# The first product on un-normed activations, 1/rms multiplied on behind PSUM

## The chip, the cores and the metric

The kernel runs on one core of a Trainium2 chip. Its time is device microseconds for one launch; a lower one is better. Five engines work on it beside each other, each in the order of its own instruction list: PE (TensorE, matmuls into PSUM), DVE (VectorE), ACT (ScalarE), POOL (GpSimd) and SP, which issues most DMA transfers. They wait for one another by semaphores, and an instruction that waits holds up all that stand behind it on its engine.

## The reference

A token block of 512 tokens with 1024 features goes through a first block (forgetting attention, a state-space branch, memory attention, gated merge) and then through two layers of a second block. What matters here is its beginning:

```python
def rms_norm(x, g):
    xf = x.astype(jnp.float32)
    y = xf * lax.rsqrt(jnp.mean(xf * xf, axis=-1, keepdims=True) + EPS)
    return (y * g.astype(jnp.float32)).astype(x.dtype)

h = rms_norm(x, g_norm[l])
z = h @ w_in[l]
q, k, v, fl, gf, u, gs, qm, gm, gl = split_cols(z)
log_f = jax.nn.log_sigmoid(fl.astype(jnp.float32) + b_forget[l].astype(jnp.float32))
y_s5 = s5_ssm(u, lam_re[l], ...)
```

The 768 columns u of the product feed the state-space branch. The 1/rms of a token is one factor for all features, so (x g) w times 1/rms is the same as (x g / rms) w.

## The kernel before, in words

Everything is feature-major: a tile is 128 features by 512 tokens. The 1024 features of x are eight tiles x[0..7]. Float32 operands are split in two parts, hi (rounded by ACT) and lo (the remainder, by DVE or POOL), and a product is three matmuls for each feature block: hi by hi, hi by lo, lo by hi (`mm3`, L105 to L110). A block of 128 output features so takes 8 x 3 = 24 matmuls of 512 columns.

Weights come in pieces of 128 by 1024 words (0.52 MB). `fetch` (L70) loads a raw piece `wr`, `split` (L79) makes `wh` on ACT (L88) and `wl` on DVE or, for every second piece, on POOL (L90). There are three buffers each of `wr`, `wh` and `wl`, so `wh` of piece n+3 can be written only when PE has read `wh` of piece n for the last time. `get` (L93) splits three pieces ahead and fetches three more. The first block's u needs pieces 0 to 5, one for each of its six output blocks; pieces 6 to 8 are for the product behind it.

The beginning (`block1`, L1457): x arrives in 16 transfers, each half of the tokens of a feature block. ACT squares it, DVE adds the squares up in `sacc` (L175). `rstd` (L192) sums `sacc` over the features with four small matmuls (L181), forms mean + eps on DVE (L199), raises it to -1/2 on POOL (L201) and spreads it over all rows in PSUM by four more (L188). `norm` then makes h: x times g times 1/rms on DVE (`hu`, L551), hi on ACT (L213), lo on DVE (L221), a half of the tokens at a time. `head` (L565) runs the first three u blocks in matmuls of 256 columns (L584, L585, L588), half by half; the other three go through `strip` and `fm` (L112) at 512 columns. `upost` (L1482) copies each block out of PSUM on ACT, reordered (L1484), and sends it through DRAM into the layout of the state-space scan.

Behind the six blocks PE goes on with `forget` (L1341), which needs all of h, and with the attention's `fv` strip (L124 to L126). On DVE the tables of the state-space branch (`s5_setup`, some 120 operations on 128 x 24 tiles, `s5t`, `s5pw`, `s5keep`) are worked in between; ACT has a table load and a sine and cosine of them (L1139, L1140).

The order on each engine is set at build time by a scheduler that merges all of this into five lists by its own estimate of the times. On the chip the lists are fixed. PSUM has eight banks: three `mm` for the blocks of a product, four `s` for small results and one `pv`.

Of the kernel before, what the change touches and what calls it, by code (L numbers as in the profile page):

```python
# [23 lines left out]
def f32(t):  # L24
    return t.bitcast(F32)


class Core:
# [17 lines left out]
    def u(self, dt=F32, name="u"):  # L46
        """a [128, 512] tile of four-byte words from the common ring."""
        self.n += 1
        return self.ring.tile([128, T], dt, tag="u", name=f"{name}_{self.n}", bufs=self.NU)
# [5 lines left out]
    def psum(self, cfg):  # L55
        """(re)divide the eight PSUM banks"""
# [36 lines left out]
    def get(self, name, kb):  # L93
        """the next piece: hi and lo as [128, kb, columns]."""
# [17 lines left out]
    def fm(self, out, w, c0, act, kb):  # L112
        """feature-major block: out[128 features, tokens] from strip columns c0..c0+128."""
        (wh, wl), (ah, al) = w, act
        for k in range(kb):
            self.mm3(out, wh[:, k, c0:c0 + 128], wl[:, k, c0:c0 + 128], ah[k], al[k], k == 0, k == kb - 1)

    def tm(self, out, ws, act, tok, cols=slice(0, 256)):
        """token-major block: out[128 tokens, cols]; ws: pieces that follow one another along k."""
# [34 lines left out]
    @staticmethod  # L154
    def half(t, hf):
        """half of the tokens: of four blocks of 128 in order, two."""
# [3 lines left out]
    def halfp(t, hf):  # L160
        """the first or second half of the tokens, in the order (t mod 4, t div 4)."""
        return t.rearrange("p (r i) -> p r i", r=4)[:, :, 64 * hf:64 * hf + 64]

    def sq_acc(self, xj, j, c=slice(0, T), name="sacc", scale=1.0):
        """sum of squares of the feature blocks, by columns."""
# [11 lines left out]
    def sumcols(self, pq, sacc, cols):  # L177
        """pq[:, i]: sums over features of the tokens of 128-blocks; cols: lists of first columns that add up."""
# [4 lines left out]
    def bcast(self, r):  # L183
        """columns r [128, n] -> [128, n * 128] in PSUM, the same in every row."""
# [7 lines left out]
    def rstd(self, sacc, cols):  # L192
        """broadcast of 1/sqrt(mean + eps), in PSUM."""
# [10 lines left out]
    def hsplit(self, src, bias=None, out=None):  # L204
        """hi, lo of src (+ bias)."""
# [20 lines left out]
class Att(Core):  # L226
    """Softmax attention on split operands. A head's logits come twice: query-major for the row
    maximum, key-major for the weights that multiply V and a block of ones, which sums them."""

    @staticmethod  # L230
    def cut(t, c):
        """columns c of t: a slice, or (i0, i1) for those of the tokens 4 i + r in the order (r, i)."""
# [5 lines left out]
    def byblock(t):  # L238
        """t, tokens 4 i + r in blocks of 128 and within these in the order (r, i), as [p, r, block, i]."""
# [3 lines left out]
    def like(t, c):  # L243
        """t in the shape of the columns c."""
        return t if isinstance(c, slice) else t.rearrange("p (r i) -> p r i", r=4)

    def split3(self, dst, src, nsh):
        """dst[..., i] (bf16, i = 0..2) add up to src (float32)."""
# [15 lines left out]
    def turn(self, mc, psum_tag):  # L264
        """columns [128 tokens, 4, 128] -> rows [128, 512] in PSUM (exact)."""
# [5 lines left out]
    def rows(self, mc, tag, psum_tag, out=None):  # L271
        """the same as bf16 in SBUF; of these the last 32 if out is given."""
# [9 lines left out]
    def unit(self, nh, sregs, tregs, qk, vsl, dst, extra=None, nq=4, hd=64, orow=None, fold=None):  # L282
        """Items of a unit of nh heads (pairs of heads share 128 rows of output).
        sregs(qb): tiles of regions (c0, n, piece, q slice, k slice, mask)
        tregs(): tiles of (regions, [(v piece, kb, columns)])
        fold(j): the tile whose other half takes the rows of -max (else these come by a product of their own)
        qk(j, piece) -> pairs (q, k); vsl(j, piece, kb) -> (hi, lo); dst(j) -> (tile AP rows, row0)"""
# [118 lines left out]
        def vrow(j):  # L406
            """rows of a head's values in its sum; the other half holds the sum of the weights."""
# [41 lines left out]
    def mix(a, b, z=1.0):  # L449
        """a and b as one list, spread evenly, b over the first part z."""  # L450
# [3 lines left out]
    def merge(self, a, b):  # L454
        """run items of a with those of b spread evenly among them."""
# [13 lines left out]
class Blk2(Att):  # L469
    def ada_gen(self, l):  # L470
        """columns [128, 48] of silu(c) @ w_ada[l] + b_ada[l]."""
# [6 lines left out]
        def fin(acc, c):  # L478
            """acc: rows of two parts, c and c + 1"""
# [36 lines left out]
    def load2(self):  # L516
        """constants of the second block"""
# [21 lines left out]
    def norm(self, x, gcols, shcols, h):  # L539
        """by half of the tokens: hi and lo of rms(x) * g + shift. Returns the stages stat, hi, lo."""  # L540
# [24 lines left out]
    def head(self, names, h, posts, norm, view, byw=False):  # L565
        """the first blocks behind a norm, a half of the tokens at a time."""
# [26 lines left out]
    def tail(self, name, act, posts):  # L593
        """the last two blocks before a norm, a half of the tokens at a time."""
# [44 lines left out]
    def put(self, o, isq, dst, scale=None, both=False, byblock=False):  # L639
        """stacks of two heads: q -> [hi;lo]; k -> [hi;hi] and lo in the rows of the head. both: q -> [hi;lo] and hi with  # L640
        the other half left to -max; k -> [hi;hi] and lo with ones for it, for heads of either half."""
# [53 lines left out]
    def pairs(q, k):  # L695
        """operand pairs whose products make up a head's logits"""
# [14 lines left out]
    def block(self, w, c0, act, kb, post):  # L711
        """one feature-major block; post(psum) may return a generator of later stages."""
# [12 lines left out]
    def strip(self, name, act, kb, posts):  # L725
        """items of feature-major blocks."""
# [12 lines left out]
    def v3(self, nb=4):  # L739
        """hi/lo token-major value tiles [128 keys, nb blocks, 128]."""  # L740
        return tuple(self.u(F32R, "v").rearrange("p (b d) -> p b d", b=nb) for _ in range(2))

    def v_new(self):
        """token-major values of two heads, in two tiles of two key blocks: hi as [v0, 1, 1, v1], lo as [v0, 0, 0, v1]."""
# [1287 lines left out]
```

## Time and profile before

| | |
|---|---|
| time, median of 3 runs | 2513.65 us (2512.61 to 2514.68) |
| span of the profiled execution, first to last instruction | 2516.8 us |
| PE busy | 2388.2 us, 95% |
| DVE, ACT, POOL busy | 61%, 41%, 32% |
| DMA | 265.28 MB, mean 105 GB/s |

The profiled execution is one of its own; its span is 3.2 us (0.13%) longer than the median of the timed runs, and its time around the span is not listed. Line numbers are those of the kernel before. In a row of the timeline the first number is the start in us from the span's start, the second the duration; brackets tell how long the engine sat idle and what released it. Matmuls overlap, so the step from one to the next is the difference of their starts, not the duration.

### The profile page before, as it was taken

What the parts mean: (1) busy time and instruction counts of PE and PEld (TensorE: products, weight loads), DVE (VectorE), ACT (ScalarE), POOL (GpSimd) and SP (SyncE); (2) the same over time, 40 slices, a digit from 0 to 9 for tenths busy, and PEclk for the clock granted to TensorE, in tenths of its full rate; (3) what the DMA queues carried; (4) which work ended last, traced back from release to release, by engine and by line L of the source; (5) the groups of instructions that cost most, each with busy time, mean ns of one, the idle gap of its engine ahead of it and who ended that gap; (6) DMA issues with size and microseconds to landing.
All of it is one profiled execution on the core that took longest, in us unless ns stands there. A gap on an engine that the chain in (4) does not pass through costs nothing. (4 is left out here: it accounts for less than half of the span.)

```text
span 2516.8 us, 32068 instructions
## 1 busy us (share of the span) xinstructions
PE 2388.2 (95%) x12162; PEld 1978.9 (79%) x12162; DVE 1533.0 (61%) x2394; ACT 1038.1 (41%) x1639; POOL 812.3 (32%) x601
## 2 busy tenths in 40 slices
PE   7999989989998889999999999998999999999999
PEld 6876778767888777787787888886777777888888
DVE  7667766666998887555459663258864726522222
ACT  4445543452333447533333423433663423423432
POOL 2445354634221552142122121227311612222121
PEclk9999999999998999998899999999999979999999
DMA  5311113213674321121138553233111313222232
GB/s 183 98 47 55 57 61 108 94 59 135 237 264 172 113 76 51 51 85 66 50 102 301 176 209 101 93 114 99 59 51 50 93 34 117 84 94 99 93 101 84
DMA packets 105610, 265.28 MB, mean 105 GB/s; under 512 B 13664, under 2 KB 23408, under 8 KB 105456
## 3 DMA queue, kind: packets, MB, share of 16 engines
q1 hardware_dynamic: 104304, 261.47, 31.2%
q8 instruction: 96, 1.57, 0.3%
q10 hardware_dynamic: 1152, 1.77, 0.2%
q14 instruction: 58, 0.48, 0.1%
HBM read 244.69 MB, written 9.44 MB: 101 GB/s over the span
## 5 line engine op out<-in xcount | busy, mean ns | idle before, releaser
L108 PE MATMUL pmm<-h,wh 128*128 128x512 f32 (+1 forms) x2232 | 855.7, 385 | 14.7 <-ACT h L213 3.9
L110 PE MATMUL pmm<-h,wl 128*128 128x512 f32 (+1 forms) x2232 | 852.9, 382 | 3.7 <-POOL wl L90 2.8
L109 PE MATMUL pmm<-l,wh 128*128 128x512 f32 (+1 forms) x2232 | 853.4, 383 | 0.0
L90 POOL TENSOR_TENSOR wl<-wr,wh 128x1024 fp32r<-128x1024 f32 (+1 forms) x173 | 422.5, 2442 | 1315.4 <-ACT wh L88 1094.4
L88 ACT CAST wh<-wr 128x1024 fp32r<-128x1024 f32 (+1 forms) x346 | 358.2, 1036 | 928.5 <-PE pmm L109 726.4
L108 PEld LDWEIGHTS pmm<-h,wh 128*128 128x128 f32 x2232 | 424.5, 190 | 96.7 <-ACT h L213 4.8
L110 PEld LDWEIGHTS pmm<-h,wl 128*128 128x128 f32 x2232 | 424.5, 190 | 82.5 <-POOL wl L90 3.8
L109 PEld LDWEIGHTS pmm<-l,wh 128*128 128x128 f32 x2232 | 425.2, 191 | 76.5 <-DVE l L221 0.7
L90 DVE TENSOR_TENSOR wl<-wr,wh 128x1024 fp32r<-128x1024 f32 (+1 forms) x173 | 225.1, 1301 | 168.9 <-ACT wh L88 166.5
L383 DVE TENSOR_TENSOR pl<-pe,ph 128x512 fp32r<-128x512 f32 (+4 forms) x168 | 121.7, 733 | 139.7 <-ACT ph L381 138.9
L961 DVE SCALAR_TENSOR_TENSOR x<-pmm,ada,x 128x512 f32<-128x512 f32 (+1 forms) x100 | 64.2, 643 | 213.9 <-PE pmm L110 213.7
L311 PE MATMUL ps<-qk,qk 128*128 128x512 f32 (+4 forms) x416 | 147.9, 386 | 16.1 <-POOL qk L672 9.6
L505 DVE SCALAR_TENSOR_TENSOR adacc<-adw,cact,adacc 128x512 f32<-128x512 f32 x168 | 154.3, 928 | 3.2 <-DMA adw<-in_wada 0.3
L221 DVE TENSOR_TENSOR l<-r,h 128x512 fp32r<-128x512 f32 x64 | 59.3, 928 | 121.6 <-ACT h L213 121.3
L379 ACT ACTIVATE pe<-ps 128x512 f32<-128x512 f32 (+4 forms) x168 | 84.5, 503 | 80.8 <-PE ps L311 72.7
L311 PEld LDWEIGHTS ps<-qk,qk 128*128 128x128 f32 x416 | 83.1, 204 | 37.7 <-POOL qk L672 11.5
L108 PE MATMUL pmm<-yh,wh 128*128 128x512 f32 (+1 forms) x244 | 94.1, 389 | 3.9 <-ACT yh L1403 2.4
L110 PE MATMUL pmm<-yh,wl 128*128 128x512 f32 (+1 forms) x244 | 93.7, 386 | 0.0
L109 PE MATMUL pmm<-yl,wh 128*128 128x512 f32 (+1 forms) x244 | 93.0, 382 | 0.0
L381 ACT CAST ph<-pe 128x512 fp32r<-128x512 f32 (+4 forms) x168 | 88.8, 528 | 9.4 <-DVE pl L383 3.5
L402 PE MATMUL ppv<-pl,v 128*128 128x512 f32 (+2 forms) x216 | 79.0, 366 | 4.1 <-DVE pl L383 4.0
L400 PE MATMUL ppv<-ph,v 128*128 128x512 f32 (+2 forms) x216 | 79.0, 366 | 2.7 <-ACT ph L381 1.6
(365 smaller groups left out, 3863.2 us busy)
## 6 DMA issues: line engine op xcount, KB each, us to landing
wr<-in_w SPq DMA_DIRECT2D x324, 512.0 KB
adw<-in_wada SPq DMA_DIRECT2D x192, 256.0 KB
xs<-xg SPq DMA_DIRECT2D x136, 64.0 KB
wr<-in_w SPq DMA_DIRECT2D x22, 384.0 KB
xd<-x SPq DMA_DIRECT2D x16, 256.0 KB
x<-xd SPq DMA_DIRECT2D x16, 256.0 KB
x<-in_x SPq DMA_DIRECT2D x16, 128.0 KB
x<-in_x SPq DMA_DIRECT2D x8, 256.0 KB
```

What stands on the lines that cost most here:

```text
L88: self.nc.scalar.copy(h[:, 0:n], r[:, 0:n])
L90: eng.tensor_tensor(out=l[:, 0:n], in0=r[:, 0:n], in1=f32(h)[:, 0:n], op=ALU.subtract)
L108: mm(out, wh, ah, start=start, stop=False)
L109: mm(out, wh, al, start=False, stop=False)
L110: mm(out, wl, ah, start=False, stop=stop)
L311: mm(outs[i] if len(r.shape) == 2 else outs[i].rearrange("p (r i) -> p r i", r=r.shape[1]), w, r, start=first and i == 0, stop=last and i ...
L379: nc.scalar.activation(out=e[:, w], in_=pt[:, w], func=AF.Exp)
L381: nc.scalar.copy(ph[:, w], e[:, w])
L383: nc.vector.tensor_tensor(out=pl[:, w], in0=e[:, w], in1=f32(ph)[:, w], op=ALU.subtract)
L400: mm(self.cut(pv, c), vh, h, start=f, stop=False)
L402: mm(self.cut(pv, c), vh, lo, start=False, stop=z)
L505: nc.vector.scalar_tensor_tensor(out=acc, in0=w, scalar=cc, in1=acc, op0=ALU.mult, op1=ALU.add)
```

## The change

x comes in eight transfers of whole feature blocks, with the first three weight pieces fetched between the first of them. From each x block, hi and lo of x times g are made directly (`rh` on ACT, `rl` on DVE), without 1/rms, into 16 tiles of their own. The first three u blocks run on these at full width, feature block by feature block over three PSUM banks of the kind `mm`. Behind them in program text come the statistics, once for all tokens, and a copy `R` of the spread 1/rms from PSUM to SBUF (ACT). `upost` multiplies by `R` as it leaves PSUM, on DVE, in place of ACT's copy. h is made after that, at full width, from x, g and `R`, for all that needs it behind u. The last three u blocks also use the un-normed tiles. The other lines that differ between the two files are comments and doc strings.

```diff
         x = [self.u(name="x") for _ in range(8)]
+        g = self.col("g_norm", 0, 8)
+        raw = [], []
         with self.tc.high_priority():
-            for hf in range(2):
-                for j in range(8):
-                    if 8 * hf + j == self.F0:
-                        self.fetch(0)
-                    nc.sync.dma_start(out=self.half(x[j], hf), in_=self.half(self.a["x"][:, j, :], hf))
-        for hf in range(2):
             for j in range(8):
-                self.sq_acc(self.half(x[j], hf), j, slice(256 * hf, 256 * hf + 256))
+                if j < 3:
+                    self.fetch(j)
+                nc.sync.dma_start(out=x[j], in_=self.a["x"][:, j, :])
+            for j in range(8):
+
+                hi, lo = self.u(F32R, "rh"), self.u(F32R, "rl")
+                nc.scalar.activation(out=hi, in_=x[j], func=AF.Copy, scale=g[:, j:j + 1])
+                self.stt(lo, x[j], g[:, j:j + 1], f32(hi), ALU.mult, ALU.subtract)
+                raw[0].append(hi)
+                raw[1].append(lo)
+        for j in range(8):
+            self.sq_acc(x[j], j)
         h = self.new_h()
-        norm = self.norm(x, self.col("g_norm", 0, 8), None, h)
...
+        R = self.u(name="R")
...
-                nc.scalar.copy(t.rearrange("p (i b) -> p b i", i=4), pm.rearrange("p (b i) -> p b i", i=4))
+                v = lambda z: z.rearrange("p (b i) -> p b i", i=4)
+                self.tt(t.rearrange("p (i b) -> p b i", i=4), v(pm), v(R), ALU.mult)
...
-        self.head(["u"] * 3, h, [upost(j) for j in range(3)],
-                  norm, self.half, True)
-        del x, norm
+        ws = [self.get("u", 8) for _ in range(3)]
+        pms = [self.p("mm") for _ in range(3)]
+        for k in range(8):
+            for (wh, wl), pm in zip(ws, pms):
+                self.mm3(pm, wh[:, k, :], wl[:, k, :], raw[0][k], raw[1][k], k == 0, k == 7)
+        pr = self.rstd(self.sums["sacc"], [[128 * b] for b in range(4)])
+        nc.scalar.copy(R, pr)
+        for j in range(3):
+            self.done(pms[j], upost(j))
+        for j in range(8):
+            t = self.u(name="hu")
+            self.stt(t, x[j], g[:, j:j + 1], R, ALU.mult, ALU.mult)
+            self.hsplit(t, None, (h[0][j], h[1][j]))
...
-        self.merge(self.strip("u", h, 8, [upost(j) for j in range(3, 6)]), [])
+        self.merge(self.strip("u", raw, 8, [upost(j) for j in range(3, 6)]), [])
```

Where it moves instructions, at three places. The number at the end of a name counts tiles and differs between the files.

POOL, the first rows behind its start. `nr` is the -1/2 power of the statistics, `wl` the lower part of a weight piece. Before:

```order
L201 TENSOR_TENSOR nr_62_206<-nv_61_204,mhalf_5_72 128x2
L90 TENSOR_TENSOR wl_76_242<-wr_74_239,wh_75_241 128x1024
L201 TENSOR_TENSOR nr_91_274<-nv_90_272,mhalf_5_72 128x2
L90 TENSOR_TENSOR wl_84_258<-wr_80_251,wh_83_257 128x1024
L90 TENSOR_TENSOR wl_120_517<-wr_82_255,wh_119_516 128x1024
```
and now, where the four `wl` are those of pieces 1, 3, 5 and 7:

```order
L90 TENSOR_TENSOR wl_72_210<-wr_26_122,wh_71_209 128x1024
L90 TENSOR_TENSOR wl_79_224<-wr_75_217,wh_78_223 128x1024
L90 TENSOR_TENSOR wl_118_411<-wr_77_221,wh_117_410 128x1024
L201 TENSOR_TENSOR nr_89_317<-nv_88_315,mhalf_5_72 128x4
L90 TENSOR_TENSOR wl_130_489<-wr_83_233,wh_129_488 128x1024
```
The one `nr` that is left stands behind the splits of pieces 1, 3 and 5; before, the two stood ahead of and behind the split of piece 1.

ACT, around the making of h (L213). Before, the second half of the tokens and the first rows behind it (`wh_83` and `wh_86` are pieces 3 and 4):

```order
L213 CAST h_41_182<-hu_93_359 128x256
L213 CAST h_42_183<-hu_94_362 128x256
L213 CAST h_43_184<-hu_95_365 128x256
L213 CAST h_44_185<-hu_96_368 128x256
L213 CAST h_45_186<-hu_97_371 128x256
L213 CAST h_46_187<-hu_98_374 128x256
L213 CAST h_47_188<-hu_99_377 128x256
L213 CAST h_48_189<-hu_100_380 128x256
L88 CAST wh_83_257<-wr_80_251 128x1024
L1484 COPY us_101_463<-ppv_57_198 128x128x4
L88 CAST wh_86_263<-wr_81_253 128x1024
L1484 COPY us_103_471<-pmm_58_199 128x128x4
```
and now, from the copy of 1/rms on (`wh_123`, `wh_129` and `wh_137` are pieces 6, 7 and 8):

```order
L1505 COPY R_68_204<-ps_90_319 128x512
L88 CAST wh_123_449<-wr_80_227 128x1024
L213 CAST h_52_188<-hu_97_349 128x512
L213 CAST h_53_189<-hu_98_353 128x512
L88 CAST wh_129_488<-wr_83_233 128x1024
L213 CAST h_54_190<-hu_99_357 128x512
L213 CAST h_55_191<-hu_100_361 128x512
L88 CAST wh_137_554<-wr_119_414 128x1024
L213 CAST h_56_192<-hu_101_365 128x512
L213 CAST h_57_193<-hu_102_369 128x512
L213 CAST h_58_194<-hu_103_373 128x512
L213 CAST h_59_195<-hu_104_377 128x512
```
The eight `h` no longer stand together: piece 6 stands ahead of all of them, piece 7 behind the second, piece 8 behind the fourth.

DVE, the lower parts of h (`l`, L221). Before:

```order
L221 TENSOR_TENSOR l_49_190<-hu_93_359,h_41_182 128x256
L221 TENSOR_TENSOR l_50_191<-hu_94_362,h_42_183 128x256
L221 TENSOR_TENSOR l_51_192<-hu_95_365,h_43_184 128x256
L221 TENSOR_TENSOR l_52_193<-hu_96_368,h_44_185 128x256
L221 TENSOR_TENSOR l_53_194<-hu_97_371,h_45_186 128x256
L221 TENSOR_TENSOR l_54_195<-hu_98_374,h_46_187 128x256
L221 TENSOR_TENSOR l_55_196<-hu_99_377,h_47_188 128x256
L1073 SCALAR_TENSOR_TENSOR s5t_181_941<-s5t_181_941,s5t_180_940 128x24
L221 TENSOR_TENSOR l_56_197<-hu_100_380,h_48_189 128x256
```
and now, from the fifth feature block to the end (`wl_138` is piece 8, `us_120` the fourth u block as it leaves PSUM):

```order
L1073 SCALAR_TENSOR_TENSOR hu_101_365<-x_21_115,cols_4_69,R_68_204 128x512
L90 TENSOR_TENSOR wl_138_555<-wr_119_414,wh_137_554 128x1024
L221 TENSOR_TENSOR l_64_200<-hu_101_365,h_56_192 128x512
L1073 SCALAR_TENSOR_TENSOR hu_102_369<-x_22_116,cols_4_69,R_68_204 128x512
L221 TENSOR_TENSOR l_65_201<-hu_102_369,h_57_193 128x512
L1073 SCALAR_TENSOR_TENSOR hu_103_373<-x_23_117,cols_4_69,R_68_204 128x512
L221 TENSOR_TENSOR l_66_202<-hu_103_373,h_58_194 128x512
L1073 SCALAR_TENSOR_TENSOR hu_104_377<-x_24_118,cols_4_69,R_68_204 128x512
L221 TENSOR_TENSOR l_67_203<-hu_104_377,h_59_195 128x512
L1070 TENSOR_TENSOR fll_108_386<-wfl_105_381,flh_107_385 128x4x12
L1070 TENSOR_TENSOR us_121_441<-pmm_120_416,R_68_204 128x128x4
L1070 TENSOR_TENSOR fll_110_392<-wfl_105_381,flh_109_391 128x4x12
```
The lower part of piece 8 stands ahead of the fifth `l`, and the multiplication of the fourth u block stands behind the last `l`.

## Rows read from the trace of the kernel before

**Rows 1.** The page, engines over the whole span: busy us (share) and instructions

```profile
PE 2388.2 (95%) x12162; PEld 1978.9 (79%) x12162; DVE 1533.0 (61%) x2394; ACT 1038.1 (41%) x1639; POOL 812.3 (32%) x601
```

**Rows 2.** Busy time per engine in four stretches; last DMA share and GB/s

```profile
0.00:20.00 20.00, 4.22 (x16) 3.55 (x16) 12.35 (x38) 11.36 (x25) 4.26 (x8) 1.00 0.79 256
...
20.00:40.00 20.00, 20.00 (x147) 20.00 (x147) 17.60 (x73) 8.97 (x17) 3.11 (x2) 1.00 0.19 66
...
0.00:2.00 2.00, 0.00 (x0) 0.00 (x0) 1.17 (x8) 0.34 (x1) 1.19 (x6) 1.00 0.08 8
...
12.00:14.00 2.00, 1.22 (x4) 0.93 (x4) 0.48 (x1) 1.56 (x3) 0.44 (x1) 1.00 1.07 411
```

**Rows 3.** Timeline of PE: start us, duration us, instruction [idle before <-releaser]

```profile
12.50 1.22 PE L188 MATMUL ps<-c,nr 128*128 128x128 f32 x4 [1.04 <-POOL nr L201]
...
25.39 0.41 PE L584 MATMUL pmm<-h,wh 128*128 128x256 f32 x1
...
26.44 0.28 PE L584 MATMUL ppv<-h,wh 128*128 128x256 f32 x1
...
39.87 0.40 PE L108 MATMUL pmm<-h,wh 128*128 128x512 f32 x1
...
56.22 0.39 PE L108 MATMUL pmm<-h,flh 128*128 128x512 f32 x1
```

**Rows 4.** Timeline of PE around a pause later in the program

```profile
560.12 0.80 PE L402 MATMUL ppv<-pl,v 128*128 128x512 f32 x1 [4.01 <-DVE pl L383]
...
562.00 0.63 PE L109 MATMUL pmm<-l,wh 128*128 128x512 f32 x1
...
562.42 0.63 PE L110 MATMUL pmm<-h,wl 128*128 128x512 f32 x1
...
565.22 0.39 PE L108 MATMUL pmm<-h,wh 128*128 128x512 f32 x1
```

**Rows 5.** Timeline of ACT, the first 75 us

```profile
15.21 1.04 ACT L88 CAST wh<-wr 128x1024 fp32r<-128x1024 f32 x1 [0.48 <-DMA wr<-in_w]
...
35.80 1.05 ACT L88 CAST wh<-wr 128x1024 fp32r<-128x1024 f32 x1 [5.74 <-PE ppv L588]
...
41.30 1.28 ACT L1139 ACT_TABLE_LOAD   x1
...
42.73 0.30 ACT L1140 ACTIVATE s5t<-s5t,hpi 128x24 f32<-128x24 f32 x1
```

**Rows 6.** Timeline of DVE, the first 75 us

```profile
16.64 2.33 DVE L175 TENSOR_TENSOR sacc<-sacc,sq 128x256 f32<-128x256 f32 x1
...
38.75 1.67 DVE L90 TENSOR_TENSOR wl<-wr,wh 128x1024 fp32r<-128x1024 f32 x1 [1.84 <-ACT wh L88]
...
44.25 0.39 DVE L1070 TENSOR_TENSOR s5t<-s5keep,s5t 128x24 f32<-128x24 f32 x2
...
48.48 1.23 DVE L90 TENSOR_TENSOR wl<-wr,wh 128x1024 fp32r<-128x1024 f32 x1
...
49.63 0.17 DVE L1070 TENSOR_TENSOR s5pw<-s5pw,s5t 128x24 f32<-128x24 f32 x1
```

**Rows 7.** Timeline of POOL, the first 75 us

```profile
11.74 0.70 POOL L201 TENSOR_TENSOR nr<-nv,mhalf 128x2 f32<-128x2 f32 x1 [10.02 <-DVE nv L199]
...
16.33 2.36 POOL L90 TENSOR_TENSOR wl<-wr,wh 128x1024 fp32r<-128x1024 f32 x1 [3.89 <-ACT wh L88]
...
36.92 2.41 POOL L90 TENSOR_TENSOR wl<-wr,wh 128x1024 fp32r<-128x1024 f32 x1 [14.55 <-ACT wh L88]
```

**Rows 8.** Groups by line and shape: count, busy us, mean ns, idle before

```profile
L1073 DVE SCALAR_TENSOR_TENSOR yl<-yf,yh 128x512 fp32r<-128x512 f32 x6 | 3.7, 684 | 0.0
...
L421 DVE TENSOR_TENSOR ym<-ppv,rb 128x512 f32<-128x512 f32 x4 | 2.7, 687 | 1.8 <-PE ppv L402 1.8
...
L213 ACT CAST h<-r 128x512 fp32r<-128x512 f32 x64 | 39.8, 621 | 2.0
...
L1484 ACT COPY us<-pmm 128x512 f32<-128x512 f32 x5 | 5.3, 1103 | 0.0
```

## The prediction, made before the changed kernel was run

> **What bounds the kernel now.** I read the page first: PE is busy 95% of the span [rows 1], so the time is PE's work plus the places where PE stands. Then the stretches: in the first 20 us PE works 4.22 us, in the next 20 all 20 [rows 2]. The change lies in this beginning, up to PE's first matmul of the forget product, the first reader of h behind u. I use that matmul as the mark: it starts at 56.22 us, and 72 matmuls earlier, at 39.87, the first three u blocks are done [rows 3]. These 72 run without a gap, 0.227 us apart. Whatever the change does to the mark passes on to the end, as PE is the bound from there on and all that follows needs h. So I sum to the mark, in the profiled execution's time, and put the difference on the median. Third, PE's timeline for its two speeds: matmuls of 256 columns take 0.41 us until 25.4 and 0.28 from 26.4 [rows 3]. It happens again later: behind a pause of 4.01 us the 512-column matmuls stand 0.42 us apart, which is 1.2 GHz, and at 565.2 they are short again (2.4 GHz) [rows 4]. The slow stretch is the 5.1 us from 560.12 on less a first matmul of 0.8: 4.3 us, ten steps of 0.42, each 0.2 too long. A pause of this length costs 2.0 us besides itself.
>
> **Removed, on PE.** 144 matmuls of half width become 72 of full width: by the step of 0.227 us, 16.35 us. Half the columns in half the step is the same work, and I cost the width itself at nothing. One of two rounds of statistics goes. The 16 half transfers of x become 8, ACT's squares run at full width under PE's first product: nothing on the path. ACT no longer copies u (1.1 us each [rows 8]); DVE does.
>
> **The first three blocks.** They no longer wait for statistics, but ACT's first `rh` stands behind the cast of weight piece 1. In front of and with that piece come 1.50 MB: two pieces of 0.52, one x block of 0.26, constants 0.19. Before, the same piece came with 3.34 MB in front of it or in it, and its cast began at 15.21 [rows 5]; the first 2 us move nothing [rows 2], so 0.255 MB/us, and 8.0 us for it now (5.7 at the 411 GB/s of 12 to 14 us [rows 2], the fast end). Cast 1.04 [rows 5], `rh` 0.62 [rows 8]: PE's first two matmuls at 9.7. The third needs `rl` from DVE. There POOL is in the way: it splits piece 1 from 9.1 to 11.5, and a DVE operation that meets such a split ends only behind it. A 256-column addition that began at 16.64, 0.3 us after POOL had begun at 16.33, took 2.33 us [rows 6, 7]. So `rl` is done at 12.2 (11.5 + 0.68 [rows 8]). Then 70 matmuls follow, the first 12 slow (0.42 each [rows 4], some 5 us as the engine comes from rest), 58 at 0.227: 12.2 + 5.1 + 13.2 = **30.5 us**, 9.4 earlier than 39.87. The last x block, behind 3.9 MB in all, is there at 17, so transfers don't hold it.
>
> **The first stall: R.** The fourth block needs a PSUM bank, and all three `mm` banks hold products that wait for R. On paper R takes 4 us; in the changed order other work stands ahead of it.
> - ACT casts pieces 3, 4 and 5 as buffers come free. All three pieces in use are read to the end now (feature block by feature block), so the first buffer is free 7 matmuls before the end: casts end at 29.95, 31.0, 32.0.
> - POOL splits piece 3 from 30.0 to 32.4 (2.4 each [rows 7]) and piece 5 to 34.8; `nr` stands behind both.
> - DVE's split of piece 4 is locked out until 32.4 (as the one at 38.75, which met POOL's of 36.92 and took 1.67 [rows 6, 7]) and ends at 33.6; then DVE is locked again until 34.8. The statistics' small operation follows at 35.0, `nr` (0.70 [rows 7]) at 35.7, the spreading on PE (1.22 [rows 3]) at 36.9.
> - ACT loads a table (1.28 [rows 5]) and makes sine and cosine by 36.9, too, then copies R: 37.5.
> - DVE has 34 table operations between the cosine and the first multiplication by R. Before, the same ones ran from 44.25 to 49.63 with a split of 1.15 in between [rows 6]: 4.2 us. So the multiplication begins at 41.1 and frees a bank at **41.8** (0.687 from PSUM [rows 8]; ACT's reordering copy took 1.1 [rows 8], the upper bound).
>
> PE pauses 11.3 us but for the small matmuls. Blocks 4 to 6: 16.35 + 2.0 for slow matmuls; they end at 49.25, 54.7 and 60.15.
>
> The Trainium skill ("SBUF — State Buffer", "SBUF: two separate sides") says that whichever of the two engines starts first holds the shared ports for its whole instruction and the other is blocked. The rows bear out one side, DVE behind POOL. By the rule DVE's split of piece 4 at 32.4, if it comes first, would also push POOL's next split, and `nr`, by 1.2 us; the sum would be 1.2 us higher.
>
> **The second stall: h.** h is made from R, from 37.5 on if nothing stood ahead. But on ACT piece 6 is ahead of the first `h`, piece 7 ahead of the third, piece 8 ahead of the fifth, and their buffers are freed by the ends of blocks 4, 5 and 6. (Such casts wait for PE now already: 5.74 us before the one at 35.80 [rows 5], but no `h` stands behind them.) On DVE `hu` and `l` alternate, each `l` waiting for ACT: 0.68 + 0.62 + 0.68 = 2.0 us for each feature block.
> - Piece 6: cast to 50.3, DVE's split to 51.5 (1.23 [rows 6]); `l` 1 and 2 at 53.5 and 55.5.
> - Piece 7: cast to 55.9 at the latest; POOL's split to 58.3 locks DVE: `l` 3 at 59.0, `l` 4 at 61.0.
> - Piece 8: cast from 60.3 to 61.4, split to 62.9; `l` 5 at 63.6, then 65.6, 67.6, 69.6.
>
> The forget product needs besides these the bank of block 4, which DVE frees behind the last `l`: 69.6 + 0.1 + 0.69. The mark is at **70.5**, 14.3 later than 56.22, behind a pause of 10.3 us, so 2.0 more for slow matmuls: **+16.3 us**. Raw weights from piece 12 on stand in SP's queue behind the u transfers of block 6, as before; three split pieces, 16 us of PE's work, cover them. I see nothing that gives the delay back: the later pauses of PE hang on its own products.
>
> On the profiled execution 2516.8 becomes 2533.1; on the median 2513.65 becomes **2530**.
>
> **Bounds.** Down: no slow matmuls behind the pauses (-4), DVE never locked out (-2.3, -2.4, -1.5), faster transfers (-2.3): +4. Up: 1.1 us for the multiplication (+0.8), longer slow phases as at the start (+2), the order of the splits (+1.2): +20. Nearest to the rows is the sum, as pauses of 4 us and locked operations are both in them. Less the fastest corner and with 3 us for a delay further on, 2519 to 2537.
>
> **Rivals.**
> - *R comes at once.* The statistics' chain is 4.4 us by itself (1.0 for the sums, 0.2, 0.7, 1.2, 0.6, 0.7). If nothing stood ahead, blocks 4 to 6 would run from 34.9 to 53.3 and h be ready by 46 (eight times 1.4 on DVE): the mark 2.9 us earlier, 4.9 if PE stays fast, 2509 to 2511. For it: PE's product does start 7 us sooner, and the scheduler's list is no slower than its operations. It decides if `nr` is done by 32.5. Against it: POOL's list, where two splits of 2.4 us stand ahead of `nr`, which none of them needs. 4%, half of it beyond 0.2%.
> - *One stall only.* R late as worked out, but h ready when block 6 ends, at 60.2: +4.0, 2517.6. It needs the casts of pieces 6 to 8 not to wait for PE; with three buffers I see no way, only that all pauses shrink together. 10%.
> - *It spreads.* The forget gates and the attention behind them come 16 us late on three engines, and the scan's u with them; if PE has no other work there, another wait of the 4 us kind [rows 4] with its slow matmuls comes on top twice: +28, 2542. 8%.
>
> **Chances.** The forecast has 78%. 0.2% is 5.0 us, about what a measurement of this kernel can tell from no change. Faster by more: 0.02. Within: 0.08, most of the second rival and the fast corner. Slower: 0.90. The range leaves out the first rival and the third, 12 in 100, and the second's better half.
>
> **What would show it.** In the new profile: PE's first 512-column matmul near 9.7 and the 72nd near 30; a pause of about 11 us whose releaser is DVE's `us`; ACT idle between R and the cast of piece 6 until block 4 ends; a second pause of about 10 us ahead of the matmuls on `flh`, released by DVE; and matmuls 0.42 apart for some 4 us behind both. A first pause under 6 us, or `h` made in one run ahead of piece 6, would prove me wrong, and so would a mark before 60.

## The result

The changed kernel took 2545.52 us (median of 4 runs, 2537.02 to 2545.94), the kernel before 2513.43 beside it: a ratio of 1.0119, interval 1.01 to 1.0137. It is slower, as forecast, but by 32 us and not by 16.3, outside the range of 2519 to 2537. Three more jobs of the same kernel gave 1.0123, 1.009 and 1.0113; in the means of the four jobs it stood 30.0, 32.5, 21.8 and 26.0 us above the kernel before. Over all jobs 22 runs of it have a mean of 2542.6 (standard error 1.4) and 115 runs of the kernel before one of 2515.1 (0.7): 27.5 us.

Single runs scatter: those of the kernel before lie between 2495.3 and 2529.4 us, and with them goes the granted clock averaged over the run (2502.58 us at 0.977, 2529.38 at 0.961; correlation -0.95, 1.9 us for 0.001). The traces of both kernels belong to runs that were a few us longer than these means (spans of 2516.8 and 2543.0 us, 26.2 apart). So places are compared in traces, and times as means.

**The profile after.** PE's timeline, the answer to [rows 3]:

```profile
9.35 1.23 PE L108 MATMUL pmm<-rh,wh 128*128 128x512 f32 x2 [9.35 <-ACT rh L1477]
11.72 0.79 PE L109 MATMUL pmm<-rl,wh 128*128 128x512 f32 x1 [1.15 <-DVE rl L1073]
...
30.54 0.95 PE L181 MATMUL ps<-c,sacc 128*128 128x1 f32 x8
37.23 2.08 PE L188 MATMUL ps<-c,nr 128*128 128x128 f32 x8 [5.75 <-POOL nr L201]
43.57 0.77 PE L108 MATMUL pmm<-rh,wh 128*128 128x512 f32 x1 [4.26 <-DVE s5pb L1183]
...
62.08 0.39 PE L110 MATMUL pmm<-rh,wl 128*128 128x512 f32 x1
73.07 0.77 PE L108 MATMUL pmm<-h,flh 128*128 128x512 f32 x1 [10.60 <-DVE fll L1070]
73.63 0.63 PE L109 MATMUL pmm<-l,flh 128*128 128x512 f32 x1
...
79.18 0.41 PE L110 MATMUL pmm<-h,fll 128*128 128x512 f32 x1
```

The first three blocks are done at 30.54, 9.3 us earlier than before. Then PE stands twice: from 30.5 to 43.57 but for the small matmuls, and 10.60 us ahead of the mark, which comes at 73.07 against 56.22: 16.85 us later. Behind it 13 steps of 0.427 us (73.63 to 79.18) cost 0.2 each, 2.6 us. The releasers named (`s5pb`, `fll`) are neighbours in DVE's list: the first stands two rows behind the multiplication `us` of the first block, the second one row behind that of the fourth (`us_121` of the list shown with the change).

ACT in the same stretch, the answer to [rows 5]:

```profile
29.15 2.94 ACT L88 CAST wh<-wr 128x1024 fp32r<-128x1024 f32 x3 [10.45 <-PE pmm L109]
...
36.22 1.28 ACT L1139 ACT_TABLE_LOAD   x1
...
39.35 0.58 ACT L1505 COPY R<-ps 128x512 f32<-128x512 f32 x1 [1.41 <-PE ps L188]
51.45 1.05 ACT L88 CAST wh<-wr 128x1024 fp32r<-128x1024 f32 x1 [11.51 <-PE pmm L109]
54.45 0.62 ACT L213 CAST h<-hu 128x512 fp32r<-128x512 f32 x1 [1.96 <-DVE hu L1073]
...
62.53 1.04 ACT L88 CAST wh<-wr 128x1024 fp32r<-128x1024 f32 x1
...
70.52 0.62 ACT L213 CAST h<-hu 128x512 fp32r<-128x512 f32 x1 [1.42 <-DVE hu L1073]
```

Behind `R` ACT stands for 11.51 us: piece 6 waits for block 4, and the first `h` stands behind piece 6. The last `h` comes at 70.52, 31 us behind `R`.

DVE, the answer to [rows 6]:

```profile
31.18 2.54 DVE L90 TENSOR_TENSOR wl<-wr,wh 128x1024 fp32r<-128x1024 f32 x1 [3.05 <-ACT wh L88]
33.64 2.31 DVE L1067 TENSOR_SCALAR s5t<-s5t 128x24 f32<-128x24 f32 x1
...
42.40 1.02 DVE L1070 TENSOR_TENSOR us<-pmm,R 128x512 f32<-128x512 f32 x1
...
59.19 2.12 DVE L221 TENSOR_TENSOR l<-hu,h 128x512 fp32r<-128x512 f32 x1 [0.69 <-ACT h L213]
...
71.90 1.02 DVE L1070 TENSOR_TENSOR us<-pmm,R 128x512 f32<-128x512 f32 x1
```

A table operation of 0.17 us takes 2.31 and an `l` of 0.69 takes 2.12: both met a split on POOL. POOL itself, the answer to [rows 7], and behind it the two splits of its first row by themselves (shortest, median and longest, in ns):

```profile
30.28 5.63 POOL L90 TENSOR_TENSOR wl<-wr,wh 128x1024 fp32r<-128x1024 f32 x2 [19.16 <-ACT wh L88]
36.17 1.01 POOL L201 TENSOR_TENSOR nr<-nv,mhalf 128x4 f32<-128x4 f32 x1 [0.26 <-DVE s5keep L1067]
58.20 2.56 POOL L90 TENSOR_TENSOR wl<-wr,wh 128x1024 fp32r<-128x1024 f32 x1 [21.02 <-ACT wh L88]
...
L90 POOL TENSOR_TENSOR wl<-wr,wh x2: 2352/2840/3327, 30.3 to 32.6; 128x1024 fp32r<-128x1024 f32 x2
```

The clock in four stretches of 10 us (the column of 0.74, 0.58, 0.78 and 0.54 is PEclk):

```profile
30.00:40.00 10.00, 3.56 (x20) 3.06 (x18) 7.90 (x33) 4.61 (x8) 6.64 (x3) 0.74 0.43 157
40.00:50.00 10.00, 6.43 (x18) 5.18 (x19) 6.08 (x27) 0.00 (x0) 0.00 (x0) 0.58 0.14 46
...
60.00:70.00 10.00, 2.47 (x11) 1.70 (x10) 7.95 (x11) 3.42 (x5) 4.65 (x13) 0.78 0.57 200
70.00:80.00 10.00, 6.93 (x18) 5.48 (x19) 4.42 (x8) 0.88 (x3) 0.00 (x0) 0.54 0.27 85
```

It falls in each pause, and PE comes out of both at 1.2 GHz: steps of 0.427 us last until 48.4 behind the first and until 79.2 behind the second.

So the beginning explains 16.85 + 2.6 = 19.4 us. The other 8 of the 27.5 lie further on. From the mark to the end, before and after:

```profile
56.22:2516.80 2460.58, 2347.80 (x11931) 1941.96 (x11929) 1489.97 (x2226) 1009.71 (x1586) 796.18 (x578) 0.97 0.31 104
...
73.07:2543.00 2469.93, 2355.26 (x11930) 1948.06 (x11930) 1494.02 (x2227) 1007.90 (x1584) 796.22 (x577) 0.96 0.31 103
```

The first number behind the comma is PE's busy time: the same matmuls take it 7.5 us more (2.6 of them the slow steps just named), and it stands idle 1.9 us longer. There the two programs have the same text, yet the scheduler made the lists anew: on PE they differ in three stretches (in the trace of before those at 202 to 225, 930 to 957 and 1781 to 1830 us), on ACT, DVE and POOL in a few places each.

### The profile page after: what moved, and what is told of

Same layout as the page of the kernel before. It is cut to its first block, busy times and chain, and to the rows that moved or that the text cites. A ratio compares the mean times of both kernels' runs of the same rounds, so it can differ in the third digit from the quotient of the medians.

```text
span 2543.0 us, 31897 instructions
## 1 busy us (share of the span) xinstructions
PE 2397.2 (94%) x12090; PEld 1981.7 (78%) x12090; DVE 1545.0 (61%) x2384; ACT 1035.0 (41%) x1626; POOL 812.9 (32%) x600
## 4 chain that ended last, share of the span: by engine, by line
PE 50%; DVE 7%; issue 4%; POOL 2%; ACT 2%; DMA 2%; SPq 1%; DVEq 0%; POOLq 0%; ACTq 0%
PE pmm L108 13%; PE pmm L109 13%; PE pmm L110 13%; PE ps L311 4%; DMA adw<-in_wada 1%; PE ppv L402 1%; PE ppv L400 1%; PE ppv L401 1%; POOL wl L90 1%; DVE unm L336 1%; DVE xs L624 1%; PE ps L617 1%; DVE adacc L505 1%; DVE wl L90 0%; POOL qv L620 0%
## 5 line engine op out<-in xcount | busy, mean ns | idle before, releaser
L110 PE MATMUL pmm<-h,wl 128*128 128x512 f32 (+1 forms) x2208 | 844.3, 383 | 3.8 <-POOL wl L90 2.8
L221 DVE TENSOR_TENSOR l<-r,h 128x512 fp32r<-128x512 f32 x64 | 59.3, 928 | 121.6 <-ACT h L213 121.3
L379 ACT ACTIVATE pe<-ps 128x512 f32<-128x512 f32 (+4 forms) x168 | 84.5, 503 | 86.5 <-PE ps L311 79.2
L336 DVE TENSOR_REDUCE unm<-ps 128x1 f32<-128x512 f32 (+2 forms) x112 | 65.0, 596 | 29.6 <-PE ps L311 29.2
```

Of the source, the lines that this page charges most:

```text
L110: mm(out, wl, ah, start=False, stop=stop)
L336: nc.vector.tensor_reduce(out=nm, in_=pts[0], axis=AX.X, op=ALU.max, negate=True)
L379: nc.scalar.activation(out=e[:, w], in_=pt[:, w], func=AF.Exp)
```

## The experiments

Each ratio is to the kernel before, run in turn with it. Line numbers of the variants are shifted by up to 18.

**r_first: the statistics first**

```diff
+        with self.tc.high_priority():
+            (sq_acc of all x, rstd)      # traced ahead of the weights
+            lead = (the sums' nv on DVE, nr on POOL)
+            nc.scalar.copy(R, pr)
+        self.lead = {i: lead for i in (3, 4, 5)}   # these splits are queued behind lead
...
-        self.s5_setup()
+        (s5_setup queued behind the third us on DVE)
```

> The changed kernel with the statistics put ahead: the sums and the power stand ahead of the splits of pieces 3 to 5 on DVE and POOL, and the state-space tables behind the first three multiplications by R. Theory (two stalls in a row, the second set by pieces 6 to 8 standing ahead of h): R at 30 to 31 instead of 39.4, PE restarts near 36 instead of 43.6, but h still waits for the ends of blocks 4 to 6, with the tables now in front of it as well, so the mark stays where it was, 71 to 75 us against 73.07, and the time at 2540 to 2547. Rival (the late R is the whole delay): the mark comes 6 to 8 us earlier, the time 2538 or less.

Ratio 1.0084 (1.0052 to 1.0116). PE:

```profile
33.64 0.47 PE L120 MATMUL pmm<-rh,wh 128*128 128x512 f32 x1 [1.85 <-DVE us L1082]
70.43 0.77 PE L120 MATMUL pmm<-h,flh 128*128 128x512 f32 x1 [20.18 <-DVE fll L1082]
```

`R` came at 31.83 and PE restarted 10 us earlier, but all except 2.6 us of that turned into a longer second pause of 20.18. R alone is not the delay. The edit made part of this pause itself: the tables now stand between the steps of h on DVE, and one of their operations took 6.29 us (45.77 to 52.06) while POOL split piece 7 and cleared tiles. The time, 2537.43 in the median, fell below the 2540 to 2547 that the theory gave.

**h_first: pieces 6 to 8 behind h**

```diff
             self.hsplit(t, None, (h[0][j], h[1][j]))
+        lead = (the last l on DVE, the last h on ACT)
+        self.lead.update({i: lead for i in (6, 7, 8)})
```

> The changed kernel with pieces 6, 7 and 8 put behind the last h on ACT and DVE, nothing else. Theory (two stalls): the first pause stays (PE restarts at 43 to 44), h is made in one run while blocks 4 to 6 are worked on, and only the weights of piece 6 and what POOL locks are left: the mark at 65 to 69 us instead of 73.07, the second pause 3 to 6 us instead of 10.6, the time 2537 to 2542. Rival (h is late only because R is): mark and time stay within 1 us.

Ratio 1.0031 (1.0008 to 1.0053), mark at 64.82:

```profile
43.10 0.76 PE L120 MATMUL pmm<-rh,wh 128*128 128x512 f32 x1 [4.26 <-DVE s5pb L1195]
64.82 0.77 PE L120 MATMUL pmm<-h,flh 128*128 128x512 f32 x1 [3.07 <-DVE us L1082]
```

With the first pause as it was, three pieces put behind h bring 8.3 us. The second stall is the order of pieces and `h`, not a late `R`. The time gained more than the mark: its mean of 2527.8 is 14.7 us below that of the changed kernel, and its median of 2525.87 lies well below the 2537 to 2542 expected.

**both: the two together**

> Both of the orders of the two kernels before it. Theory: the gains add up only now, the mark at 61 to 65 us, still later than the 56.22 of the kernel before the change since PE waits for wl of piece 3 (all three pieces end together) and DVE has h, three multiplications and splits locked by POOL in a row: time 2530 to 2536. On the loss behind the mark (9 us more between the two profiles): if it goes with the pauses and the clock behind them, this kernel loses under 5 us behind the mark against the kernel before; if it comes of the order that the scheduler gives the later program, it has no reason to shrink and may be anything from -3 to +10.

Ratio 1.001 (0.9985 to 1.0035), restart at 34.06, mark at 62.53. The mark gains only 2.3 us more than in h_first: PE now waits 11.86 us, since table operations stand between the steps of h on DVE, and behind the last `l` (done at 57.6) a split and a table operation that met POOL's split of piece 7 (59.10, 2.33 us) stand ahead of the multiplication that frees the bank. The time was again lower than the 2530 to 2536 expected.

**nr_first: of r_first only the statistics**

> Of the kernel r_first only the first half: the statistics' sums and power ahead of the splits, the state-space tables left where the scheduler puts them, ahead of the multiplications by R. It parts the first stall in two. Theory (tables and splits each hold the first multiplication up): the power at 31 us instead of 36.2, but sine, cosine and the 34 table operations still stand in front of the multiplication, so PE restarts at 39 to 43, little better than 43.57 and well behind the 33.64 of r_first. Rival (the splits alone made R late): PE restarts at 34 to 36.

One run, 2533.08 us. `R` at 34.53, restart at 38.38, mark at 71.55. The restart lies between the two theories. DVE ahead of it:

```profile
32.74 2.24 DVE L1148 TENSOR_SCALAR s5keep<-s5t 128x24 f32<-128x24 f32 x1
34.90 2.40 DVE L1200 TENSOR_SCALAR s5keep<-s5keep 128x24 f32<-128x24 f32 x2
37.21 1.02 DVE L1082 TENSOR_TENSOR us<-pmm,R 128x512 f32<-128x512 f32 x1
```

Against what was expected, the scheduler put the first multiplication ahead of the 34 table operations here. What kept it from 35.1, when `R` was done, to 37.21 were two other table operations, each held up by one of POOL's two splits (32.61 to 37.26). So this run doesn't price the 34 operations.

**both_dve: the splits of pieces 1, 3 and 5 on DVE**

```diff
-        eng = self.nc.gpsimd if i % self.WP == self.WP - 1 else self.nc.vector
+        eng = self.nc.gpsimd if i > 5 and i % self.WP == self.WP - 1 else self.nc.vector
```

> The kernel both (statistics ahead, h ahead of pieces 6 to 8) with the splits of pieces 1, 3 and 5 on DVE instead of POOL. It prices the locking of DVE by POOL's splits in the first 40 us. Theory (DVE stands while POOL splits, and two such splits, 4.9 us, run ahead of wl of piece 3 and of h): PE's second group of matmuls 1.5 to 2.5 us earlier, the restart behind the third block at 31.5 to 33, the mark 2.5 to 5 us earlier than the 62.53 of both. Rival (POOL's time is covered, DVE only gets more work): mark within 1 us of 62.53 or later.

One run, 2501.67 us, at a granted clock of 0.973, so only its trace counts: PE's third matmul starts at 10.70 instead of 11.71, the restart is at 32.85, the mark at 59.26, 3.3 us earlier than in both. The first gain is smaller than the 1.5 to 2.5 us expected. A split of 1.2 us on DVE is cheaper here than one of 2.4 on POOL that stops DVE.

**normed: full width without un-norming**

```diff
-                (rh and rl from x)
+        raw = h
+            (rstd, R, h at full width: ahead of the weights)
-                self.tt(t.rearrange(...), v(pm), v(R), ALU.mult)
+                nc.scalar.copy(t.rearrange(...), pm.rearrange(...))
```

> The changed kernel without its un-normed product: x in 8 transfers, statistics once over all tokens, h made at full width first, and all six u blocks from h at full width over the same three banks, copied out by ACT as before the change. It parts the change in two. Theory (full width by itself costs the half that the kernel before could start on; un-norming gives it back): PE's first u matmul at 22 to 26 us against 9.35 with un-normed x and 16.6 before the change, no pause of over 3 us before the mark, the mark at 58 to 63 us, so 2 to 7 later than before and 10 to 15 earlier than in the changed kernel; time 2 to 7 us above the kernel before. Rival (the late buffers of three blocks that end together are the trouble, whatever x is): a pause of over 5 us behind the third block here too, mark beyond 65.

Ratio 1.0031 (1.0008 to 1.0054). First u matmul at 24.66, no pause over 1 us behind it, although three blocks end together here, too, mark at 63.80, a little outside 58 to 63. Un-norming lets PE start 15 us earlier, and the changed kernel is 9 us later at the mark all the same.

**best2 and best3: un-normed u without the two stalls**

```diff
-        pms = [self.p("mm") for _ in range(3)]
+        pms = [self.p("pv"), self.p("mm"), self.p("mm")]
-        for k in range(8): (three blocks, feature block by feature block)
+        for k in range(4): (three blocks, feature block by feature block)
+        (block 0: k = 4; statistics; k = 5 to 7; copy of R; then blocks 1 and 2: k = 4 to 7)
...
+        (hu of j+1 ahead of l of j; pieces 6 to 8 and s5_setup behind the last l)
+        (splits of pieces 1, 3, 5 on DVE; in best3 that of piece 7, too)
```

> Un-normed x for u, full width and 8 transfers as in the changed kernel, but: statistics in the middle of the first three blocks, which are finished one after the other from the fifth feature block on (so that their weight buffers come free one by one); first block in the pv bank; splits of pieces 1, 3 and 5 on DVE, not POOL; h ahead of pieces 6 to 8 and its steps staggered on DVE; tables behind h. Theory: R at 26 to 28, no pause of over 2 us before the mark, the mark at 48 to 51 us, 5 to 8 earlier than the 56.22 of the kernel before the change; time 2505 to 2512. Rival (the later order decides more than the beginning): the mark comes early and the time is still 2513 to 2520.

Ratio 0.9971 (0.9949 to 0.9993): a little faster than both kernels, 8.5 us below the kernel before in the means. It changes several things at once, and no run parts what each brings. `R` at 25.92, one pause:

```profile
49.67 0.75 PE L120 MATMUL pmm<-h,flh 128*128 128x512 f32 x1 [1.99 <-DVE s5t L1085]
```

What held it, on DVE:

```profile
43.34 1.47 DVE L233 TENSOR_TENSOR l<-hu,h 128x512 fp32r<-128x512 f32 x2
...
46.21 2.85 DVE L1093 TENSOR_SCALAR s5t<-s5t 128x24 f32<-128x24 f32 x1
48.48 1.04 DVE L1082 TENSOR_TENSOR us<-pmm,R 128x512 f32<-128x512 f32 x1
```

h was whole at 44.8; the bank came late, as `us` stood behind a table operation that met POOL's split of piece 7.

> The kernel best2 with the split of piece 7 on DVE, too, so that no split of POOL runs before the mark. Theory (in best2 h was ready at 44.8 us; a table operation of DVE at 46.21 then waited 2.7 us for POOL's split, and the multiplication that frees the bank stood behind it): the pause of 2.0 us ahead of the mark is under 0.8, the mark at 47.3 to 48.3 instead of 49.67, the time 1 to 4 us below that of best2 and 6 to 12 below the kernel before. Rival (PE waits for something else there, a bank or flh): mark within 0.5 us of 49.67.

Ratio 0.9989 (0.9968 to 1.001). The pause shrank to 1.09 us, now ahead of `flh`, which ACT casts behind pieces 6 to 8, and the mark came at 48.74, not 47.3 to 48.3. The time did not follow: 2510.1 in the mean against 2507.6, each measured beside other runs of the kernel before, and 3.8 us below those against 8.5.

**after_again, late, hold8, hold16: where the rest is lost**

> The changed kernel once more, unaltered, in more runs beside the kernel before: in the four runs of the first measurement it stood 32 us above the kernel before, of which its trace shows 16.85 at the mark and 2 to 3 in slow matmuls right behind it. Theory (the other 13 us are the granted clock of those few runs, which moves by itself: the kernel before alone ran from 2501.18 to 2529.38 in 29 runs, at 0.977 to 0.961): over more runs the difference is 17 to 24 us, a ratio of 1.007 to 1.0095, and mark and pauses in the trace stay within 1 us. Rival (the change makes the later program slower): 28 to 34 us again, a ratio over 1.011, with the time from the mark to the end 8 us or more above that of the kernel before at like clocks.

Ratio 1.0123 (1.0097 to 1.0148), mark at 72.02. The 32 us were not the chance of four runs alone.

```diff
+            for j in range(16):
+                nc.sync.dma_start(out=x[j % 8], in_=self.a["x"][:, j % 8, :])     # late
```

> The kernel before the change, with x loaded three times over (16 transfers of 256 KB more in front), so that everything starts later, without a pause of PE in the middle of u; the scheduler's order of the later program is not word for word that of the kernel before. Theory (behind the mark only the clock of the run decides): the mark 13 to 18 us later, the time later by the same 13 to 18 us, no more than 3 us of difference from mark to end in the means. Rival (any shift makes the scheduler order the later program worse): 6 us or more on top of the shift of the mark.

Ratio 1.0073 (1.0048 to 1.0099): the mark 9.5 us later (65.7), less than I had worked out, the time 20 us (error 2.8) above the mean of the kernel before in that job, as the rival had it.

```diff
+        for i in range(30):                      # hold16; 15 in hold8
+            if i: nc.vector.wait_ge(sem, i)
+            nc.vector.memset(hold.ap(), 0.0).then_inc(sem, 1)
```

> The kernel before the change with the same lists of instructions on all engines; only DVE works through 15 memsets of a PSUM bank, one behind the other, before its first instruction, so that PE's start is put off while ACT and the transfers run ahead. No pause of PE is added behind its start. Theory (behind the mark the program takes what it takes, a like list gives a like time): the mark 5 to 9 us later, the time later by as much, within 3 us. Rival (the time behind the mark goes up with the delay itself, whatever the lists): 4 us or more on top, as in the kernel with x loaded three times, which lost 9.5 us at the mark and 18 in time.

> The same with 30 memsets. Theory: mark and time both 13 to 18 us later, the two within 3 us. Rival: 5 to 12 us on top of the mark's delay, as in the changed kernel (16 to 17 at the mark, 32 in time).

Ratios 1.0016 (0.999 to 1.0042) and 1.0068 (1.0041 to 1.0094). The marks came at 60.12 and 68.74, 3.9 and 12.5 us later, both a little short of what was expected; the means are 4.5 and 15.8 us above that of all runs of the kernel before, and 5.7 and 17.0 (errors 2.4 and 2.1) above those of the same job. With like lists a delay costs itself and 1 to 5 us more, while `late`, with lists made anew, paid twice its delay.

**tail and best_tail: the later lists of before**

```diff
         mixer_kernel(tc, out, **args)
+        for s in ORDER:      # about 800 instructions, in the order of the kernel before
+            for p, q in zip(s, s[1:]): (q is queued behind p, without a wait)
```

> The changed kernel with its own beginning, both pauses included, but behind about 110 us every engine's list in the order of the kernel before (edges between some 800 instructions; on PE the list is then the one of before from its 149th row on, without exception). In 10 runs the changed kernel lost 32 us, 16 to 17 of them at the mark and 2.6 in slow matmuls right behind it; 13 lie further on. Theory (these 13 are the order of the later lists, which the scheduler made anew): the time falls to 17 to 22 us above the kernel before, 10 to 13 below the changed kernel beside it, with mark and pauses unchanged. Rival (they come from the two long pauses or the delay, whatever the later order): still 28 to 34 above the kernel before, within 4 us of the changed kernel.

> The changed kernel itself, beside the one with the later lists of before, on the same chip and in turn with it. Both theories: 28 to 35 us above the kernel before, as in the ten runs so far (32). If it came out at 17 to 24 here, the ten runs would have been chance.

> The changed kernel with the later lists of before, once more: in 8 runs it stood 19 us above the mean of all runs of the kernel before so far (2515.2), the changed kernel 28 in 16 runs. Theory (the later lists cost the changed kernel some 9 us): again 7 to 11 us below the changed kernel in the means. Rival (chance): within 4 us of it.

> The changed kernel, in turn with the one before it: 26 to 32 us above the kernel before, in the means.

tail: 1.0066 (1.0043 to 1.0088) and 1.007 (1.0044 to 1.0097), in the means 14.5 and 17.8 us above the kernel before. The changed kernel beside it: 1.009 (1.0061 to 1.0119) and 1.0113 (1.0069 to 1.0158), in the means 21.8 and 26.0 us, the first of them less than expected, with the mark at 72.29 and 71.71. The beginning of tail is that of the changed kernel:

```profile
43.55 0.77 PE L108 MATMUL pmm<-rh,wh 128*128 128x512 f32 x1 [4.25 <-DVE s5pb L1183]
73.11 0.77 PE L108 MATMUL pmm<-h,flh 128*128 128x512 f32 x1 [10.60 <-DVE fll L1070]
```

Over all runs tail has 2533.3 us (20 runs, error 1.3), 18.2 above the kernel before and 9.3 (error 1.9) below the changed kernel. The kernel before has means from 2512.1 to 2520.0 in the several jobs, so pairs within one job are the safer numbers: tail is 7.3 and 8.2 below the changed kernel, 7.7 together (error 2.7), where the theory had 10 to 13 and then 7 to 11. So behind this beginning the lists that the scheduler made anew behind 110 us cost 8 to 9 us, and 16 to 18 are left for the beginning, where the trace shows 19.4.

> best3 (mark at 48.7, 7.5 us earlier than in the kernel before) with the later lists of the kernel before on every engine, on PE from row 1007 on. Theory: the whole gain at the mark arrives at the end, 6 to 11 us below the kernel before, 0.996 to 0.9975. Rival (best3's own later lists cost nothing, its 3.8 us in the means were chance): within 3 us of best3's time, 2510.

Ratio 1.0012 (0.999 to 1.0034), 2517.4 us in the mean, 7.3 above best3 (2510.1; 6.4, error 2.7, by the kernel before beside each), with the mark at 48.79. The theory fails here: the lists of before, put behind an earlier beginning, cost 6 to 7 us instead of bringing some. The order of before is not the better one as such.

Nor is the new order dear as such. By the names and shapes in their traces, `both` and `normed` have the changed kernel's lists on every engine from 265 us on, the second and third stretch included. In the means of their jobs they stand 3.5 and 8.1 us above the kernel before (errors 2.9 and 2.6), and their marks 6.3 and 7.6 us later: within these errors they lose nothing behind the mark. So what costs the changed kernel 8 to 9 us is the order of its first stretch, or its lists together with its beginning. No run parts these.

## Why the prediction was wrong

**Right, and its sizes.** PE's first matmul was to come at 9.7 (9.35), dense work from 12.2 (11.72), the three blocks at 30.5 (30.54; this close by luck, as the work began 0.5 us sooner and took 0.5 longer). POOL's two splits stood ahead of `nr`, DVE's table operations ahead of the first multiplication, pieces 6, 7 and 8 ahead of the first, third and fifth `h`, each as read from the lists, and h_first and r_first show that these orders make the two stalls; how the first divides between splits and tables is not shown. The pause ahead of the mark was to be 10.3 us (10.60), with slow matmuls behind both pauses.

**Short by 2.6 us at the mark** (70.5 forecast, 73.07 found), in small terms. POOL's second split lasted 3.33 us by its own row, not 2.4: DVE's split of piece 4, begun at 31.18 while POOL worked, ended at 33.72 (31.18 + 2.54). That is the half of the rule of which the prediction had no row (the Trainium skill, "SBUF — State Buffer", "SBUF: two separate sides"), and the trace agrees: most of the 1.2 us that the prediction left out for it is there. DVE's next table operation was held until 35.95, the cosine came at 37.9 instead of 36.9, and the first multiplication began at 42.40, not 41.1. It took 1.02 us, not 0.687, and so did that of the fourth block: the row of the reordering copy, 1.1, which the prediction kept as the upper bound, was the nearer one. The slow matmuls cost 2.4 instead of 2.0 behind the first pause and 2.6 behind the mark. `R` itself was ready at 39.9 instead of 37.5, since `nr` on four columns took 1.01, not the 0.70 of two, and the spreading 2.08, not 1.22: that row was of four matmuls, and now there are eight. This cost nothing, as the multiplication stood behind the tables for 2.5 us more. All this stays inside the range: 19.4 us.

**The step that failed** is the sentence "I see nothing that gives the delay back: the later pauses of PE hang on its own products", with 3 us at the most for all that lies further on. The runs show some 8 there: 27.5 in all, less 19.4. The prediction took the program behind the mark for one piece that is only moved ("Whatever the change does to the mark passes on to the end"). The text of that part is the same, but the order of its instructions isn't: the scheduler, which starts from another beginning, ordered three later stretches of PE's list anew. tail gives these stretches back the order of before and wins 7.7 us beside the changed kernel (error 2.7; 9.3 over all runs), beginning and pauses unchanged. I had compared the lists only where the change lies. That the order alone would do it is not shown, since `both` and `normed` have the same lists from 265 us on at no cost.

**Not the rivals either.** The first two are out: `nr` was done at 37.18, not by 32.5, and the last `l` at 71.86, 9.5 us behind the end of block 6. The third had the time nearly right (2542), by new waits of PE. But behind the mark PE stands 112.8 us in the trace of before and 114.7 in that of after, while its busy time goes from 2347.80 to 2355.26 at a granted clock of 0.97 and 0.96. What differs in these two traces is how much of the same work runs at 1.2 GHz, and the granted clock goes with the time between runs of one kernel, too. Why the changed kernel gets more of the low clock stays open: best_tail, `both` and `normed` show that neither order is better by itself.

**The base.** I put a difference within the profiled execution on a median of 3 runs, as if each were good to 0.2%. Runs of this kernel lie up to 0.8% from their mean, so that part of the first 32 us is the draw of 4 and 4 runs; 27.5 is the better number. It still is 4 us above the upper end that I allowed for.

## What to carry over

Where a scheduler orders the work, compare the lists of the whole program, not of the changed place alone: a change at the beginning can reorder a stretch 900 us later. What that costs is for runs to tell: 8 to 9 us behind one beginning, nothing behind two others. Work that is ready sooner gains nothing while other work stands ahead of it in its engine's list: ask for each row of the new list what stands ahead of it, and what that waits for. Three blocks that end together are no fault by themselves (`normed` has them and no pause); it is a fault where what frees their banks or the next weights stands behind something late.

## Not expected of the hardware

The time of a one-core kernel moved by 34 us over 111 runs, along its granted clock. DVE and POOL hold each other up in both directions: 2.31 us for a table operation of 0.17 on DVE, and 3.33 for a split of 2.4 on POOL. Yet not every operation of DVE is held: in r_first two multiplications of a PSUM tile by `R` took 1.97 us together, from 32.45 on, in the midst of POOL's two splits (30.55 to 35.44, 2.4 each).
